# Output operands unsplit in DRAM, V's copies in the output phase, and an earlier set of early products in a hybrid attention and SSD layer

## The chip, the cores and the metric

The kernel runs on one core of a Trainium2 chip. A core has five engines with a queue of instructions each: PE (TensorE, matmuls; its weight loads are shown as PEld), DVE (VectorE), ACT (ScalarE), POOL (GpSimd) and SP (SyncE). SP, ACT and POOL also issue DMA transfers, and 16 DMA engines carry these out between DRAM, SBUF and DRAM again. The metric is the device time of one execution in microseconds, the lower the better. All data are float32.

## The reference

One decoder layer on x of 2048 tokens by 1024 features:

```python
proj = x @ w_in                            # 1024 -> 6672
q, k, v, z_att, z_ssm, xbc, dt_raw = split(proj)
# attention: 16 heads of 64, window of 128 steps, dilations 1, 4, 16, ALiBi bias
o_i, lse_i = dilated_window_attention(q, k, v, dilation_i)
y_att = sum_i softmax_i(lse)[i] * o_i
y_att = rms_norm(y_att * silu(z_att), g_att)
# SSM: causal convolution of width 4, Mamba-2 scan in chunks of 128
xs, B, C = split(silu(conv(xbc)));  dt = softplus(dt_raw + bias)
y_ssm = rms_norm((ssd(xs, dt, a, B, C) + d * xs) * silu(z_ssm), g_ssm)
out = concat(y_att, y_ssm) @ w_out         # 2048 -> 1024
return layer_norm(alpha * x + out)
```

## The kernel before

**Products in three parts.** A float32 product is made from three matmuls on a faster float32 type. Each operand a is split into a high part h (a cast, on ACT) and a low part l = a − h (a subtraction, on DVE or POOL), and h·h, h·l and l·h are added in PSUM. Who splits, when, and whether the split or the whole operand lies in DRAM is what much of this change is about.

**Stages.** First V is projected and stored (0 to 210 us of the profiled execution). Then 52 jobs follow, which make all other projections and the SSM half of the output projection. Then come the attention of eight head pairs (1481 to 2017 us) and the tail: the attention half of the output projection for 16 row blocks of 128 tokens, the norms and the result (to 2250 us).

**Jobs.** A job makes a 2 by 2 set of blocks by a scheme of seven products (a Strassen-like one, whose operands are sums and differences of blocks, named B11, B21, B22, T1 to T4). Each product is 12 matmuls of 128x512, so a job is 84. `products` (L391) issues them; `keep` (L402 to 405) copies a PSUM bank to an `ev` tile on ACT, one of six. The jobs go through the token halves: jobs 0 to 9 for half 0, jobs 10 to 31 for half 1, jobs 32 to 43 for half 0 again, and jobs 44 to 51 are the output jobs. A job's kind says which columns it makes: c (convolution channels), s (`z_ssm`), q, k, z (the attention gate) and o. In jobs 0 to 9 the order is c, s, c, s, c, s, c, s, c, c, and job 12 is an s job too. From about count 161 the SSM scan runs between the jobs.

**What sets the order.** PE, DVE, ACT and POOL run in the order in which the program is written; SP's order is found by the compiler's scheduler. Beside the seven products of a job the program puts small pieces of other work. `later[n]` (with its helpers `after` and `put`) is a list of functions for count n, and `flush()` (L386) runs those of the present count after each product. Job m covers counts 7m to 7m + 6. At 19 us a job, one count is 2.7 us.

**The pieces the change touches.** `token_sums` (L145) makes the sums for token half 1, and `output_side` (L270) those for the output jobs, from the weights `wout` and their gains. Both go through `in_steps` (L119): a difference, the high part on ACT (L127, L129), the low part on DVE (L134, L136) and a store of both (L139), each at a count of its own. The operands of the output jobs have four `wot` tiles, and POOL issues their stores. `output_load` (L307) loads the high and low parts of each of the seven operands, 1 MB each, on POOL (L320). `token_side` (L302) does the same for a new token half. `fin_zs` (L459) applies the gate function to a block of `z_ssm` and gathers it in a tile `ez`, of which there is one, and stores it (L468), twice in a job. `copy_v` (L580) copies V inside DRAM into the orders that dilations 4 and 16 read. `load_qk` (L783) loads queries and keys of a head pair. `fin_o` (L715) adds the rows of x (`row_load`, L707, on ACT's queue) to the SSM half.

**Attention and tail.** A pair has 24 half-steps, numbered (dilation, quarter, half). `scores` (matmul L953), `transposes` and `values` (L1002) run in a pipeline. While a pair runs, `combine` (L1064) adds the three dilations of the pair before with their weights: L1078 multiplies, L1087 adds, L1093 applies the gate, and L1098 and L1099 split the first three row blocks of the result (`uh`), which go to DRAM as `d_uh`. In the tail `product_early` (L1183) makes the part of row blocks 0 to 2 that needs no pair 7, from what `fetch_early` (L1131) brings back from `d_uh`; row block 3 is split in SBUF. `product_last` (L1199) adds pair 7. `gate` (L1260) multiplies pair 7's dilation 0 on POOL. `gather` and `weights` (L1047 to L1059) make the weights of the three dilations.

## Time and profile before

| | us |
|---|---|
| time, median of 3 runs | 2246.71 (2243.5 to 2250.11) |
| the profiled execution | 2251.73 |
| its span, first to last instruction | 2250.0 |
| PE busy | 2059.8 (92 % of the span) |
| DVE busy | 1487.2 (66 %) |
| ACT busy | 1216.9 (54 %) |
| POOL busy | 1184.1 (53 %) |

The mean granted clock of TensorE is 0.957 of full speed. The DMA engines moved 551.79 MB. Of the 16 engines' time, SP's queue took 35.7 %, POOL's 24.9 % and ACT's 14.1 %. A view by slices cuts the span into 40 equal parts and gives a busy share in tenths for each. A list of waits gives, for each engine, what ended its idle time: the engine, tile and line that waited, the releaser, then us in total, number and longest. A row of the timeline gives the start, the duration and, in brackets, the idle time ahead of the instruction and what released it.

### The profile page before, as it was taken

The page shows a single profiled execution, that of the slowest core. Times are in us where ns is not written, and L with a number is a line of the kernel's source. Part 1 is how long each engine was busy: PE and PEld are TensorE (multiplying, and loading weights), DVE is VectorE, ACT ScalarE, POOL GpSimd, SP SyncE. Part 2 cuts the span into 40 slices and gives each one's busy share as a digit, 9 for nine tenths or more (in the row PEclk, how much of TensorE's full clock was granted, in tenths as well). Part 3 has the DMA queues.
Part 4 walks back from the last instruction along what each step waited for, and adds up shares of the span by engine and source line. Part 5 has one row for each costly group of instructions (what it writes and reads, how often), then busy time and mean ns, then how long its engine had stood idle before and what let it go on. Part 6 is the DMA issues. An engine that isn't in the chain of part 4 may idle for free. (4 is left out here: it accounts for less than half of the span.)

```text
span 2250.0 us, 39433 instructions
## 1 busy us (share of the span) xinstructions
PE 2059.8 (92%) x13768; PEld 1707.0 (76%) x13768; DVE 1487.2 (66%) x3252; ACT 1216.9 (54%) x3131; POOL 1184.1 (53%) x980
## 2 busy tenths in 40 slices
PE   7999988879998999989999989979999999978798
PEld 7998766657887777767777868868887778866686
DVE  3432756837899678665656436548887888875666
ACT  3331443425555676666666534447887888862332
POOL 2113445745777667664555335532466677751544
PEclk9999999989999999999999999979999999998899
DMA  9999778886858868799788894453777778788342
GB/s 328 368 328 333 240 228 287 303 310 186 227 177 299 305 248 290 244 358 338 241 262 272 288 363 159 156 200 125 205 219 178 223 222 231 217 258 248 127 131 87
DMA packets 291799, 551.79 MB, mean 245 GB/s; under 512 B 77936, under 2 KB 145136, under 8 KB 274832
## 3 DMA queue, kind: packets, MB, share of 16 engines
q1 hardware_dynamic: 201536, 252.77, 35.7%
q0 software_dynamic: 36192, 194.46, 24.9%
q10 hardware_dynamic: 53872, 102.05, 14.1%
q8 instruction: 109, 1.79, 0.3%
q14 instruction: 90, 0.74, 0.1%
HBM read 359.39 MB, written 206.57 MB: 252 GB/s over the span
## 5 line engine op out<-in xcount | busy, mean ns | idle before, releaser
L351 POOL TENSOR_TENSOR w<-wr,w 128x512 fp32r<-128x512 f32 x287 | 432.2, 1520 | 291.5 <-ACT w L350 199.1
L969 ACT ACTIVATE P<-P,st 128x256 f32<-128x256 f32 (+1 forms) x768 | 345.1, 451 | 114.9 <-DVE st L961 114.4
L961 DVE CUSTOM_DVE_ANT_0 P<-S,tb 128x256 f32<-128x256 f32 (+1 forms) x768 | 235.3, 362 | 87.7 <-PE S L953 50.9
L404 ACT COPY ev<-pp 128x512 f32<-128x512 f32 x208 | 120.9, 581 | 254.8 <-PE pp L399 163.6
L350 ACT CAST w<-wr 128x512 fp32r<-128x512 f32 x287 | 171.1, 618 | 54.2 <-DVE wr L343 34.7
L343 DVE TENSOR_TENSOR wr<-wr 128x512 f32<-128x512 f32 x164 | 181.6, 1107 | 24.5 <-DMA wr<-w 12.6
L984 DVE COPY PT<-T 128x512 f32<-128x512 f32 (+1 forms) x304 | 196.6, 677 | 1.6 <-PE T L982 1.5
L982 PE MATMUL T<-ident,P 128*128 128x128 f32 x1200 | 179.6, 287 | 5.1 <-DVE PT L984 4.8
L1002 PE MATMUL N<-PT,v 128*64 128x128 f32 x2400 | 178.0, 286 | 3.4 <-DMA v<-d_v 3.1
L412 DVE TENSOR_TENSOR ev<-pp,ev 128x512 f32<-128x512 f32 x184 | 121.9, 682 | 74.2 <-PE pp L399 54.0
L1002 PEld LDWEIGHTS N<-PT,v 128*64 128x64 f32 x2400 | 130.7, 139 | 36.8 <-issue 25.7
L982 PEld LDWEIGHTS T<-ident,P 128*128 128x128 f32 x1200 | 130.6, 143 | 29.5 <-DVE PT L984 6.2
L1078 POOL TENSOR_TENSOR wb<-num,wb 128x2048 f32<-128x2048 f32 x21 | 96.4, 4591 | 102.7 <-DMA wb<-d_wd 73.0
L969 ACT ACTIVATION_READ_ACCUMULATOR P<-P,st 128x1 f32 x768 | 143.8, 187 | 0.0
L953 PE MATMUL S<-kh,qp 64*128 64x256 f32 (+1 forms) x1024 | 126.1, 306 | 0.0
L395 PE MATMUL pp<-TB22h,w 128*128 128x512 f32 x208 | 89.5, 430 | 36.5 <-ACT ev L404 34.4
L503 DVE SCALAR_TENSOR_TENSOR acc<-U,cw,acc 128x2048 f32<-128x2048 f32 x36 | 114.0, 3167 | 6.2 <-ACT acc L500 5.8
L452 DVE SCALAR_TENSOR_TENSOR ev<-ev 128x512 f32<-128x512 f32 x64 | 71.1, 1125 | 70.1 <-ACT ev L451 70.0
L953 PEld LDWEIGHTS S<-kh,qp 64*128 64x128 f32 x1024 | 88.8, 188 | 22.0 <-issue 20.5
L194 PE MATMUL pp<-vh,xh 128*128 128x256 f32 (+1 forms) x320 | 90.9, 290 | 15.8 <-ACT xh L217 15.8
L187 POOL TENSOR_TENSOR vl<-vraw,vh 128x256 fp32r<-128x256 f32 (+1 forms) x32 | 29.9, 938 | 130.9 <-ACT vh L186 107.7
L397 PE MATMUL pp<-TB22l,w 128*128 128x512 f32 x208 | 87.8, 422 | 5.2 <-DMA TB22l<-d_T0B 2.1
(487 smaller groups left out, 6106.6 us busy)
## 6 DMA issues: line engine op xcount, KB each, us to landing
wr<-w ACTq DMA_DIRECT2D x157, 256.0 KB
v<-d_v POOLq DMA_DIRECT2D x24, 1024.0 KB, 7.6
d_wc<-w SPq DMA_DIRECT2D x44, 512.0 KB
w<-d_wc POOLq DMA_DIRECT2D x44, 512.0 KB, 5.9
wb<-d_wd SPq DMA_DIRECT2D x42, 512.0 KB
csb<-d_cs ACTq DMA_DIRECT2D x32, 512.0 KB
st<-xT SPq DMA_DIRECT2D x23, 512.0 KB
d_v<-vt SPq DMA_DIRECT2D x16, 512.0 KB
```

Of the source, the lines that this page charges most:

```text
L343: tt = lambda o, a, b, op=OP.subtract: nc.vector.tensor_tensor(q[o], q[a], q[b], op=op)
L350: nc.scalar.copy(t[:, 0], q[nm])
L351: nc.gpsimd.tensor_tensor(t[:, 1], q[nm], t[:, 0].bitcast(F32), op=OP.subtract)
L404: nc.scalar.copy(e, ps)
L412: nc.vector.tensor_tensor(e, a, e, op=op)
L503: return lambda: nc.vector.scalar_tensor_tensor(acc[0], U[:, j:j + 16, :], cw[:, i, j:j + 1], acc[0], op0=OP.mult, op1=OP.add)
L953: nc.tensor.matmul(ov(sp[h][:, 256 * b:256 * b + w]), A["q"][d][x][hr, blk], kv(A["k"][y][hr]), start=(m == 0), stop=(m == 2))
L961: nc.vector.tensor_tensor_reduce(P[:, h, b, 256 - w:256], sp[h][:, c0:c0 + w], tab[:, h, tab.shape[2] - w:], 1.0, 3.0e38, OP.add, OP.min, ...
L969: nc.scalar.activation(p, p, AF.Exp, bias=stat(A, 0, d, h, blk), scale=-1.0, accum_out=stat(A, 1, d, h, blk))
L982: nc.tensor.transpose(tp[:, h, b], P[:, h, b, 128 * which:128 * which + 128], ident)
L984: nc.vector.tensor_copy(pt[:, :, bl[0]:2], tp[:, :, bl[0]:2])
L1002: nc.tensor.matmul(nm[64 * h:64 * h + 64, bq * 128:bq * 128 + 128], v[:, k, 64 * h:64 * h + 64], pts[which][:, h, b], start=(f or not whic ...
```

## The change

It has five parts. (1) The operands of the output jobs are stored whole (`d_U` has no high and low part any more). `output_side` makes each in one instruction into its own tile (13 tiles `wo`) and stores 256 KB on SP, at counts 45 to 67 instead of 38 to 66. `output_load` is now three functions: `load` brings an operand of 1 MB on SP into one of two staging tiles, `high` casts it on ACT (L316), `low` subtracts on DVE, or on POOL for operands 2 and 5 (L321). The token sums have two `to` tiles instead of three and two counts per sum. (2) `fin_zs` keeps both halves of a job in one `ez` tile and stores once, in runs of 512 bytes. (3) The 32 copies of V, 512 KB each, move from counts 3 to 149 to counts 318 to 356. (4) The queries of pair 0 are loaded at the first count of job 50 and the keys at the first count of job 51. Before, all four loads stood at the second count of job 51. (5) `d_uh` holds six pairs. The early products of row blocks 0 to 2 are of pairs 0 to 5; pair 6 stays in its tile `uh` and is multiplied with pair 7 in `product_last`. The steps of pair 6's `combine` move from half-steps (0,3,0), (1,0,0), (1,1,0), (1,2,0) of pair 7 to (1,0,1), (1,1,0), (1,2,0), (1,3,1).

POOL at the change of token half, ahead of job 10, before. L351 splits weights, L302 loads an operand of token half 1, L139 stores an operand of the output jobs:

```order
L139 DMA d_UB_143<-wot 128x2x512
L351 TENSOR_TENSOR w<-wr,w 128x512
L302 DMA TB11h<-d_T1B_116 128x2048
L302 DMA TB11l<-d_T1B_116 128x2048
L139 DMA d_UB_142<-wot 128x2x512
L351 TENSOR_TENSOR w<-wr,w 128x512 x2
L302 DMA TT1h<-d_T1T_119 128x2048
L302 DMA TT1l<-d_T1T_119 128x2048
L139 DMA d_UT_144<-wot 128x2x512
```

And now (L353 and L295 are the same two lines):

```order
L353 TENSOR_TENSOR w<-wr,w 128x512 x62
L295 DMA TB11h<-d_T1B_116 128x2048
L295 DMA TB11l<-d_T1B_116 128x2048
L353 TENSOR_TENSOR w<-wr,w 128x512 x2
L295 DMA TT1h<-d_T1T_119 128x2048
L295 DMA TT1l<-d_T1T_119 128x2048
```

The stores of the output operands and the copies of V have left POOL here.

POOL at the end of the output jobs, before. L790 loads queries and keys, L895 a table, L897 V:

```order
L351 TENSOR_TENSOR w<-wr,w 128x512 x53
L790 DMA qh<-d_qh_60 128x2048
L790 DMA kh<-d_kh_76 128x2048
L790 DMA ql<-d_ql_68 128x2048
L790 DMA kl<-d_kl_84 128x2048
L895 DMA tb_13252<-tabs 128x2x128
L897 DMA v<-d_v_100 128x16x128
```

And now (L584 copies V, L799 loads queries and keys, L902 and L904 are table and V):

```order
L799 DMA qh<-d_qh_60 128x2048
L799 DMA ql<-d_ql_68 128x2048
L584 DMA d_v_102<-d_v_100 16x8192
L353 TENSOR_TENSOR w<-wr,w 128x512 x3
L584 DMA d_v_102<-d_v_100 16x8192
L353 TENSOR_TENSOR w<-wr,w 128x512
L584 DMA d_v_102<-d_v_100 16x8192 x2
L353 TENSOR_TENSOR w<-wr,w 128x512
L584 DMA d_v_102<-d_v_100 16x8192
L353 TENSOR_TENSOR w<-wr,w 128x512
L799 DMA kh<-d_kh_76 128x2048
L799 DMA kl<-d_kl_84 128x2048
```

The queries stand ahead of the last copies and the keys right behind them, and the weight splits are cut into pieces by the copies.

POOL in the last pair, before. L1116 loads final weights, L1078 and L1087 are steps of pair 6's `combine`, L897 loads V for dilation 16:

```order
L1116 DMA kh<-d_wo 128x2048
L1116 DMA kl<-d_wo 128x2048
L1078 TENSOR_TENSOR wb<-num,wb 128x2048
L897 DMA v<-d_v_102 128x16x128
L1078 TENSOR_TENSOR wb<-num,wb 128x2048
L1087 TENSOR_TENSOR wb<-wb 128x2048
L1116 DMA qh<-d_wo 128x2048
```

And now (seven lines further down in the file):

```order
L1123 DMA kh<-d_wo 128x2048
L1123 DMA kl<-d_wo 128x2048
L904 DMA v<-d_v_102 128x16x128
L1123 DMA qh<-d_wo 128x2048
L1123 DMA ql<-d_wo 128x2048
L1123 DMA v<-d_wo 128x2048
L1321 DMA num<-d_za_99 128x2048
L1085 TENSOR_TENSOR wb<-num,wb 128x2048 x2
L1094 TENSOR_TENSOR wb<-wb 128x2048
```

V's load and the loads of the final weights stand ahead of the first step of `combine`.

The diff, without the parts that the text above tells in full:

```diff
-    d_U = {n: dtile(f"d_U{n}", [2, 128, 4, 512]) for n in ("B11", "B21", "B22", "T1", "T2", "T3", "T4")}
+    d_U = {n: dtile(f"d_U{n}", [128, 4, 512]) for n in ("B11", "B21", "B22", "T1", "T2", "T3", "T4")}
-    d_uh = dtile("d_uh", [3, 128, 2, 7, 128])
+    d_uh = dtile("d_uh", [3, 128, 2, 6, 128])
...
+            def item(nm, make):
+                def f():
+                    make(tile_(nm))
+                    nc.sync.dma_start(d_U[nm][:, k], R[nm])
+                return f
...
+                (0, "B11", lambda o: act(o, R["11"], AF.Copy, scale=col(gc, 0))),
+                (0, "B22", lambda o: act(o, R["22"], AF.Copy, scale=col(gc, 1))),
+                (1, "B21", lambda o: act(o, R["21"], AF.Copy, scale=col(gc, 1))),
+                (2, "T1", lambda o: stt(o, R["12"], col(gc, 0), R["B11"], op0=OP.mult, op1=OP.subtract)),
+                (3, "T3", lambda o: stt(o, R["12"], col(gn, 0), R["B22"], op0=OP.mult, op1=OP.add)),
+                (3, "T2", lambda o: tt(o, R["B22"], R["T1"], op=OP.subtract)),
+                (4, "T4", lambda o: tt(o, R["T2"], R["B21"], op=OP.subtract))):
+                put(b + n, item(nm, make))
...
+            def load(i):
+                stage[i] = qq.tile([128, NR, NJ], F32, name="q" + "hl"[i % 2], bufs=1).rearrange(
+                    "p (k r) j -> p k (r j)", k=4)
+                nc.sync.dma_start(stage[i].rearrange("p k t -> p (k t)"), d_U[LEFT[i]].rearrange("p k t -> p (k t)"))
+            def high(i):
...
+                for h in range(2):
+                    nc.scalar.copy(T[i][0][:, 2 * h:2 * h + 2], stage[i][:, 2 * h:2 * h + 2])
+            def low(i):
+                for h in range(2):
+                    s = slice(2 * h, 2 * h + 2)
+                    (nc.gpsimd if i in (2, 5) else nc.vector).tensor_tensor(
+                        T[i][1][:, s], stage[i][:, s], T[i][0][:, s].bitcast(F32), op=OP.subtract)
...
+            n0 = 7 * 43
+            for i in range(7):
+                c = n0 + 3 * i // 2 if i else n0 - 4
+                put(c, lambda i=i: o_high(i))
+                put(c + 1, lambda i=i: o_low(i))
+                if i < 5:
+                    put(c + 1, lambda i=i: o_load(i + 2))
+            o_load(0)
+            o_load(1)
...
-            for j in range(32):
-                later.setdefault(4 * j + (3 if j < 13 else 25), []).append(lambda j=j: copy_v(1 + j // 16, j % 16))
+                put(7 * 45 + 3 + 5 * j // 4, lambda j=j: copy_v(1 + j // 16, j % 16))
...
-                    after(1, lambda: load_qk(pairs[0]))
+                    later[count[0]].insert(0, lambda: load_qk(pairs[0], 1))
+                if m + 2 == len(jobs):
+                    after(0, lambda: load_qk(pairs[0], 0))
...
-            nc.gpsimd.dma_start(SP[n].rearrange("p (a c t) -> p a c t", a=2, t=128)[:, :, 0:7], d_uh[n])
+            nc.gpsimd.dma_start(SP[n].rearrange("p (a c t) -> p a c t", a=2, t=128)[:, :, 0:6], d_uh[n])
...
-                mm(pss[hf], hf, lhs, range(6), True, False)
-            for hf in range(2):
-                mm(pss[hf], hf, lhs, [6], False, True)
+                mm(pss[hf], hf, lambda e: (part(t, 0)[:, e, :], part(t, 1)[:, e, :]), range(7 if n == 3 else 6),
+                   True, True)
...
-                mm(pss[hf], hf, lambda e: (e7[:, 0, n], e7[:, 1, n]), [7], True, True)
+                mm(pss[hf], hf, lambda e: (two[e - 6][:, 0, n], two[e - 6][:, 1, n]), [7] if n == 3 else [6, 7],
+                   True, True)
...
-                        step = ((0, 3, 0), (1, 0, 0), (1, 1, 0), (1, 2, 0))
+                        step = ((1, 0, 1), (1, 1, 0), (1, 2, 0), (1, 3, 1))
```

121 lines of the change are left out of this document (45 added, 76 removed).

## The prediction

> **What bounds the kernel now.** I read first the page's slices, then the waits, and then cut the span into the jobs that the change touches.
>
> ```profile
> PE   7999988879998999989999989979999999978798
> ...
> PEclk9999999989999999999999999979999999998899
> ```
>
> Each digit is 1/40 of the span (56.25 us). PE is busy nearly everywhere, so time is lost only in the few slices below 9. They are the early jobs (slices 6 to 9), the start of the attention (slice 27) and the tail (from slice 37). The list of all waits names what stands there:
>
> ```profile
> ACT ez L465 <- DMA d_zs<-ez: 45.3, 7, 12.4
> ...
> PE pp L395 <- ACT ev L404: 42.6, 12, 9.1
> ...
> ACT wot L127 <- DMA d_UB<-wot: 22.2, 6, 8.7
> ```
>
> The columns are us in total, times, longest. ACT waits for a *store*: its result tile (`ez`, `wot`) is still being written to DRAM. PE in turn waits for ACT, because the PSUM bank of the next product is emptied by ACT's copy L404, which is queued behind the waiting instruction. The stretches that hold these jobs, with one quiet job ahead as a measure, are:
>
> ```profile
> 232.00:251.00 19.00, 19.00 (x85) 15.72 (x85) 12.97 (x16) 10.41 (x18) 10.21 (x10) 1.00 0.70 242
> 251.00:279.00 28.00, 22.84 (x89) 18.28 (x88) 24.70 (x41) 12.77 (x22) 11.58 (x9) 0.88 0.70 214
> 299.00:330.00 31.00, 22.11 (x85) 17.68 (x85) 17.47 (x20) 10.42 (x19) 11.99 (x9) 0.83 0.71 214
> 349.00:379.00 30.00, 20.88 (x86) 16.82 (x85) 19.79 (x20) 12.39 (x24) 18.06 (x18) 0.83 0.83 277
> 400.00:427.00 27.00, 21.60 (x87) 17.12 (x86) 23.09 (x22) 14.35 (x26) 16.94 (x16) 0.94 0.82 262
> 446.00:493.00 47.00, 29.88 (x85) 20.54 (x85) 9.97 (x13) 10.28 (x17) 21.36 (x27) 0.78 1.02 389
> 512.00:538.00 26.00, 21.58 (x84) 17.29 (x83) 15.34 (x13) 11.91 (x21) 14.30 (x14) 0.87 0.75 213
> 1276.00:1302.00 26.00, 21.71 (x90) 17.52 (x89) 5.49 (x10) 6.30 (x11) 8.78 (x12) 0.93 1.08 390
> 1321.00:1347.00 26.00, 21.68 (x86) 16.85 (x85) 7.81 (x11) 8.47 (x15) 8.88 (x8) 0.93 0.98 375
> 1349.00:1481.00 132.00, 131.89 (x579) 108.24 (x577) 72.50 (x79) 57.99 (x100) 64.50 (x49) 1.00 0.50 166
> ```
>
> Columns: stretch, us, busy time of PE, PEld, DVE, ACT, POOL, granted clock, DMA share, GB/s. A job is 84 matmuls of 128x512; the first row does it in 19.0 us with no gap at full clock. Everything above 19.0 is loss, and it includes the lower clock that follows a gap. The losses in row order are 9, 12, 11, 8 (jobs 2, 4, 6, 8), 28 (job 10, the change of token half), 7 (job 12), 7 and 7 (jobs 42 and 44, into the output jobs). The seven output jobs behind (last row) lose nothing, with the DMA half idle.
>
> **Part by part, 1: output operands unsplit, one `ez` tile.** Before, each operand of the output product is split on ACT and DVE at counts 38 to 66 of the schedule, and POOL stores 512 KB per piece. Now 256 KB per piece go out on SP at counts 45 to 67, from 13 tiles instead of 4; an `ez` store happens once per job, in 512-byte runs instead of 256-byte ones.
>
> ```profile
> ACT wot L129 <- DMA d_UT<-wot: 10.9, 7, 4.0
> ...
> 317.11 1.15 ACT L465 ACTIVATE ez<-ev 128x512 f32<-128x512 f32 x2 [12.38 <-DMA d_zs<-ez]
> ...
> 525.70 0.63 ACT L465 ACTIVATE ez<-ev 128x512 f32<-128x512 f32 x1 [9.77 <-DMA d_zs<-ez]
> ```
>
> The waits of ACT named so far (`ez` up to 45.3, `wot` 22.2 + 10.9) cover the 40 us lost in jobs 2, 4, 6 and 8. The second `ez` tile of a job waited for the first one's store, 12.38 us; now the next user of the tile is the next z job, over 19 us later, so that wait is gone. With 13 tiles no `wot` piece waits for its own store. I take −35 of the 40. The bounds are −42 (also small losses of the jobs between) and −22 (about half, if other ACT work such as the token sums, now with two tiles and not three, takes over the place). Job 12 has one `ez` wait, 9.77 us: −7 (−7 to 0).
>
> **2: change of token half (job 10).** POOL loads 14 pieces of 1 MB for job 10, and before, the last 512 KB operand stores stood between them on POOL.
>
> ```profile
> 435.58 0.57 POOL L302 DMA_DIRECT2D TB11h<-d_T1B  x1
> ...
> 488.80 0.79 PE L397 MATMUL pp<-TT3l,w 128*128 128x512 f32 x1 [1.99 <-DMA TT3l<-d_T1T]
> ```
>
> First issue to last piece used: 53 us for 14.7 MB, with the engines at share 1.02. So it is bound by bytes: what goes away is the four last stores, 2.1 MB, at 389 GB/s 5.4 us, and POOL's wait ahead of the first issue, some 5 us (the splits in front follow ACT, which no longer stalls). −10, from −6 to −13; the rest of the 28 stays, since the loads still begin when the old half's tiles come free.
>
> **3: V copies moved.** 32 copies of 512 KB, DRAM to DRAM, are 16.8 MB.
>
> ```profile
> d_v<-d_v POOLq DMA_DIRECT2D x16, 512.0 KB, 5.5
> ```
>
> Their removal from counts 3 to 149 frees DMA time up to job 21: −3 (0 to −8) for store waits there. They now run at counts 318 to 356, in the output jobs 45 to 51. In the last window row those jobs move 166 GB/s at share 0.50, so full share is about 332 GB/s; the copies are 51 us of it, put into some 109 us that had half free, 54 us. It fits, but barely: share about 0.97. What hides it is the idle half; where the x rows or split weights of a job come late behind copies, the price shows. The two rows at share 1.08 and 0.98 lost 7 us per job, most of it for reasons of part 4. I take +6, from 0 to +25 (half of seven times 7).
>
> **4: output operands split at use.** Seven 1 MB loads on SP into two staging tiles, then two ACT casts and two subtractions each (DVE; POOL for i = 2 and 5) of 128x1024. Half the bytes of before, but new work:
>
> ```profile
> L218 DVE TENSOR_TENSOR xl<-st,xh 128x1024 fp32r<-128x1024 f32 x15 | 18.5, 1231 | 38.8 <-ACT xh L217 38.8
> ...
> L1255 POOL TENSOR_TENSOR kh<-kh,wb 128x1024 f32<-128x1024 f32 x8 | 23.5, 2938 | 0.6
> ...
> 1289.92 0.59 ACT L404 COPY ev<-pp 128x512 f32<-128x512 f32 x1 [6.73 <-DMA d_qh<-ev]
> ```
>
> DVE: 10 × 1.23 = 12.3 us; POOL: 4 × 2.94 = 11.8 us; ACT about as DVE. In the two windows these engines are busy 5 to 9 of 26 us, so the work itself is hidden. Not hidden is a late load: if a staging tile is not full, ACT waits in `high`, and behind it L404 and so PE; on SP a load that waits for its staging tile holds the q and k stores behind it, which free `ev` (the 6.73 us wait above is of that kind). Against it stands that half of the operand bytes leave this stretch, at 390 GB/s 19 us of DMA (7 of 14 MB). Bounds −6 (one of the two losses goes) to +14 (both double); I take +4, since two staging tiles are few.
>
> **5: start of the attention.** Queries are now loaded in job 50, keys at the first count of job 51.
>
> ```profile
> 1483.52 1.20 POOL L897 DMA_DIRECT2D v<-d_v  x1 [8.29 <-ACT ev L718]
> ...
> 1489.32 0.48 PE L953 MATMUL S<-kl,qh 64*128 64x128 f32 x2 [7.59 <-DMA kl<-d_kl]
> 1489.95 6.87 DVE L719 SCALAR_TENSOR_TENSOR ev<-x,ev 128x512 f32<-128x512 f32 x1 [5.81 <-DMA x<-xc]
> 1497.00:1518.00 21.00, 20.70 (x136) 16.32 (x136) 11.26 (x70) 13.94 (x65) 0.85 (x2) 0.50 0.21 62
> 1518.00:1526.00 8.00, 8.00 (x56) 6.35 (x56) 3.25 (x18) 4.08 (x19) 0.00 (x0) 0.50 0.06 17
> ```
>
> The wait for `kl` (7.59) goes: keys land before job 51 ends. The last x row also comes sooner (5.81), since no q and k traffic stands beside it, and L719 no longer runs beside POOL's casts of `qp`. Late next is V of pair 0, issued at 1483.52 behind the last output row, and 7 us under way. The first scores start about 1485 instead of 1497, the first values product a little after: −11. Bounds −8 (V decides alone) and −22 (also 10 us of the half clock, below). The Trainium skill ("GPSIMD Engine Reference", 1. Specifications) says that POOL shares its SBUF interfaces with VectorE, in contention with DVE instructions that have two SBUF inputs. This trace agrees, 6.87 us for L719; it speaks against `low` of i = 2 and 5 on POOL, and by it part 4 would be an estimated 2 to 6 us dearer, inside its bounds.
>
> **6: last pair and tail.** Pair 6's weighting moves two to three half-steps later, so the load of V for dilation 16 no longer stands behind it on POOL:
>
> ```profile
> 1984.39 4.57 POOL L1078 TENSOR_TENSOR wb<-num,wb 128x2048 f32<-128x2048 f32 x1 [17.31 <-DMA wb<-d_wd]
> ...
> PE N L1002 <- DMA v<-d_v: 3.1, 1, 3.1
> ```
>
> −3. The tail's early products now need only pairs 0 to 5, long stored:
>
> ```profile
> 2030.85 4.52 POOL L1260 TENSOR_TENSOR num<-num 128x2048 f32<-128x2048 f32 x1
> 2031.67 3.76 DVE L1047 TENSOR_TENSOR mm<-cm 128x32 f32<-128x32 f32 x1 [15.56 <-DMA cm<-d_st]
> 2034.06 0.76 PE L1172 MATMUL S<-kh,num 128*128 128x512 f32 x1 [16.72 <-DMA num<-d_uh]
> ...
> 2056.65 1.07 ACT L1197 COPY qp<-S 128x512 f32<-128x512 f32 x2 [20.39 <-DMA wb<-d_wd]
> ...
> 2121.73 0.79 PE L1172 MATMUL S<-kh,num 128*128 128x512 f32 x1 [11.27 <-ACT num L1142]
> 2034.00:2076.00 42.00, 41.39 (x171) 33.19 (x171) 23.85 (x22) 9.57 (x16) 2.64 (x3) 0.95 0.80 237
> 2124.00:2250.00 126.00, 116.80 (x498) 93.98 (x498) 83.26 (x120) 36.33 (x51) 60.46 (x22) 0.96 0.36 119
> ```
>
> PE's 16.72 us wait goes, yet I count it at almost nothing. What ends the tail's first part is pair 7's own chain: statistics (2031.67, 15.56 us behind their store), weights, ACT held till 2056.65 by its 20.39 us wait, then the product and the row blocks, where PE waits 11.27 us again. Work begun sooner on PE only makes PE wait longer there. From that chain only the 3.76 us go, which a 128x32 instruction costs beside L1260 on POOL: −3. Pair 6 adds 18 matmuls to the late part, 18 × 0.23 = 4.1 us, which those waits mostly hide: +1.5. Behind 2124 PE is busy 116.80 of 126 and nothing changes. Tail and pair 7: −4.5, from −16 (the early begin pays after all) to +4 (the 18 matmuls are not hidden).
>
> **Sum.** −35 − 7 − 10 − 3 + 6 + 4 − 11 − 4.5 = −60.5 us on the span of 2250.0, so 2189.5. The profiled execution took 2251.73, 5 us above the median of 2246.71, and I take the difference from the median: 2246.7 − 60.5 = **2186 us**.
>
> **Rivals.** (a) *The stalls are partly replaced.* For it speaks that ACT has several kinds of store waits behind one another in the early jobs, so that the next one takes over; part 1 then brings −22, part 4 costs +14, part 3 +10: 2186 + 13 + 10 + 4 = 2213. Against it: the stores become half as large and the tiles three times as many. (b) *The clock returns at once at the start of the attention.* In the two rows of 1497 to 1526 the granted clock is 0.50 while PE is busy 28.70 of 29 us. With the full clock ACT would bound that work, 13.94 + 4.08 = 18 us, so 11 us go: 2175. Against it: this trace shows 29 us of half clock under unbroken work. The Trainium skill ("TensorE: Matmul & The Clock Gate", What's actually happening) says that about 3.4 us of sustained activity give the full clock back. By that rule the result would be this rival's; the trace does not agree, as the rows above show, so it has a small chance. (c) *The early begin pays in full:* the tail is PE-bound from 2017 on, 16.7 − 4.1 = 12.6 us instead of 1.5: 2175. Against it: PE's 11.27 us wait at 2121.73. (d) *The copies starve the output jobs; slower.* Its place is jobs 45 to 51, its mechanism that x rows and weights queue behind the V copies at a share near 1. The three rows at share 0.98 to 1.08 lost 7, 7 and 28 us, on average 14; seven such jobs cost 98 instead of 6: 2278. It decides from about 9 us per job on, where 66 us eat the gain. Against it: on average 3 % of the DMA stays free, and the copies are spaced one per 3.4 us.
>
> **Chances.** Forecast 0.58, (a) 0.19, (b) 0.14, (c) 0.05, (d) 0.04. A measurement of this kernel tells about 0.3 %, 6.7 us, from no change. Faster by more: 0.93 (all but (d) and a far tail of (a)); within: 0.03; slower: 0.04. Range 2158 to 2222: down to the bounds −42 and −22 of parts 1 and 5 with the rest as taken, less 10; up over (a) with another 9 us of copies.
>
> **What would show it.** Part 1: no `ez` or operand wait on ACT of over 2 us, windows of jobs 2 to 8 at 19 to 21 us. Part 2: job 10 near 37 us. Part 3: share 0.9 to 1.0 in the output jobs and PE still without gaps; gaps before L395 that name x rows or weights show (d). Part 4: ACT waits in the casts of the staged loads. Part 5: first score product right behind job 51, V of pair 0 the last to come. Part 6: no wait for `d_uh`, a longer one at the later row blocks, and the same distance from the end of the attention to the end. It is wrong if early jobs keep more than 20 of their 40 us, or if the output jobs lose over 4 us each.

## The result and the profile after

The changed kernel takes 2225.44 us (median of 4 runs, 2220.32 to 2228.08) against 2247.08 us. The ratio is 0.990, with an interval of 0.988 to 0.993. It is faster, by 21.6 us, but the forecast was 60.5 us, and the time lies above the top of the range (2222). The profiled execution has a span of 2226.3 us against 2250.0.

The stretches of the changed kernel that answer to those shown of before, with the same columns (stretch, us, busy PE, PEld, DVE, ACT, POOL, granted clock, DMA share, GB/s), are job 2, job 4, job 10, job 12, job 42, job 44, and jobs 45 to 51 together:

```profile
252.00:280.00 28.00, 22.94 (x92) 18.50 (x91) 24.52 (x41) 12.08 (x22) 10.01 (x8) 0.88 0.57 177
299.00:318.00 19.00, 19.00 (x86) 15.78 (x85) 12.83 (x17) 9.10 (x18) 9.83 (x8) 1.00 0.84 280
413.50:455.00 41.50, 27.40 (x85) 19.97 (x84) 5.53 (x10) 8.39 (x13) 16.36 (x20) 0.81 1.01 383
475.00:494.00 19.00, 19.00 (x85) 15.77 (x84) 14.74 (x13) 10.57 (x17) 14.08 (x13) 1.00 0.66 205
1230.00:1249.00 19.00, 19.00 (x86) 15.76 (x85) 3.64 (x7) 6.73 (x11) 5.22 (x7) 1.00 0.95 345
1272.00:1304.00 32.00, 22.06 (x85) 17.57 (x84) 20.35 (x14) 15.28 (x23) 21.16 (x10) 0.79 0.47 164
1304.00:1456.00 152.00, 137.02 (x589) 110.70 (x587) 82.28 (x85) 60.49 (x104) 84.13 (x85) 0.98 0.80 279
```

Jobs 4, 12 and 42 run without a gap now. Job 2 still loses 8 us, and job 44 more than before. The last row is the surprise: seven output jobs that lost nothing before lose 18 us, and the DMA engines are busy only 0.80 of that time. The whole account, from the first matmul of each job and the first values product of each pair, in both traces:

| stretch | before, us | after, us | difference | forecast |
|---|---|---|---|---|
| V stage and jobs 0 to 9 | 445.6 | 413.5 | −32 | −35 |
| jobs 10 and 11 | 66.2 | 61.3 | −5 | −10 |
| job 12 | 26.3 | 19.0 | −7 | −7 |
| jobs 13 to 41 | 738.1 | 736.3 | −2 | −3 |
| jobs 42 to 44 | 70.3 | 73.8 | +3.5 | +4 |
| jobs 45 to 51 | 134.3 | 152.3 | +18 | +6 |
| end of job 51 to the first values product | 21.9 | 11.9 | −10 | −11 |
| pairs 0 to 6 | 453.8 | 460.2 | +6.4 | none |
| pair 7 | 60.7 | 68.2 | +7.5 | −3 |
| tail | 232.8 | 229.7 | −3 | −1.5 |

Three rows carry 29 of the 37 us that are missing on the span: the output jobs (12), pairs 0 to 6 (6.4) and pair 7 (10.5). Job 10 (5) and the early jobs (3) stand behind them. The waits that stand in those places in the changed kernel are, of DVE over the whole span, and of ACT in job 2 (timeline):

```profile
DVE ev L719 <- DMA x<-xc: 29.8, 9, 6.3
```

```profile
272.19 0.62 ACT L137 CAST to<-st 128x512 fp32r<-128x512 f32 x1 [8.87 <-DVE st L143]
```

In the output jobs it is the x rows that come late, on DVE; ACT's next use of the `ev` tiles and PE's bank stand behind that. In job 2 ACT waits for DVE in a token sum, not for a store. Pair 7 has a wait that was not there before (timeline rows of POOL, ACT and PE):

```profile
1966.64 4.58 POOL L1085 TENSOR_TENSOR wb<-num,wb 128x2048 f32<-128x2048 f32 x1 [22.17 <-ACT num L1016]
...
1980.53 4.50 POOL L1085 TENSOR_TENSOR wb<-num,wb 128x2048 f32<-128x2048 f32 x1
```

```profile
1985.06 0.59 ACT L1019 COPY num<-N 128x512 f32<-128x512 f32 x1 [13.19 <-POOL wb L1085]
```

```profile
1986.20 0.47 PE L989 MATMUL T<-ident,P 128*128 128x128 f32 x1 [8.10 <-ACT P L976]
```

ACT may not write pair 7's result for dilation 16 into the `num` tile until POOL has read pair 6's from it. POOL's first multiplication begins 38 us into pair 7 (1928.4); before it began 28 us into it (1984.39 against 1956.4). Why it is later stands on SP's queue, where the weights go to DRAM (L1065, L1058 before) and are loaded back once they have landed (L1071, L1064), first of the changed kernel, then of before:

```profile
1940.93 0.36 SPq L1065 DMA_DIRECT2D d_wd<-cm  x1
1955.84 1.32 SPq L1071 DMA_DIRECT2D wb<-d_wd  x2
```

```profile
1969.34 0.36 SPq L1058 DMA_DIRECT2D d_wd<-cm  x1
1977.03 1.12 SPq L1064 DMA_DIRECT2D wb<-d_wd  x2
```

The small store took 14.9 us to land instead of 7.7. In the changed kernel POOL does not wait for it ahead of its loads, and has issued 7 MB of them from 1935 to 1945: five final weights, V and the gate. Before, two weights were on the way at that time.

The row of POOL names an ACT copy as its releaser, where other traces name the loaded weights, so the link to the store rests on a comparison of traces and on the run below that moves the loads. In nine traces with the late steps and the loads ahead of them, the store was 11.0 to 16.5 us under way and the first multiplication began 38 to 44 us into pair 7. In three of the kernel before it was 5.5 to 8.0 us, and 26 to 29 us.

### The profile page after: what moved, and what is told of

The parts are those of the page before. It is cut to its first block, busy times and chain, and to the rows that moved or that the text cites. A ratio compares the mean times of both kernels' runs of the same rounds, so it can differ in the third digit from the quotient of the medians.

```text
span 2226.3 us, 39336 instructions
## 1 busy us (share of the span) xinstructions
PE 2056.8 (92%) x13768; PEld 1708.8 (77%) x13768; DVE 1460.6 (66%) x3234; ACT 1219.3 (55%) x3125; POOL 1173.1 (53%) x942
## 5 line engine op out<-in xcount | busy, mean ns | idle before, releaser
L353 POOL TENSOR_TENSOR w<-wr,w 128x512 fp32r<-128x512 f32 x287 | 436.6, 1538 | 284.4 <-ACT w L352 201.2
L991 DVE COPY PT<-T 128x512 f32<-128x512 f32 (+1 forms) x304 | 197.0, 678 | 12.5 <-PE T L989 12.5
L345 DVE TENSOR_TENSOR wr<-wr 128x512 f32<-128x512 f32 x164 | 169.0, 1031 | 22.6 <-DMA wr<-d_us 9.6
L1085 POOL TENSOR_TENSOR wb<-num,wb 128x2048 f32<-128x2048 f32 x21 | 96.1, 4577 | 110.2 <-DMA wb<-d_wd 72.7
L454 DVE SCALAR_TENSOR_TENSOR ev<-ev 128x512 f32<-128x512 f32 x64 | 73.5, 1161 | 68.8 <-ACT ev L453 68.7
L397 PE MATMUL pp<-TT2h,w 128*128 128x512 f32 x208 | 84.0, 404 | 15.0 <-ACT ev L406 15.0
L397 PE MATMUL pp<-TB21h,w 128*128 128x512 f32 x208 | 84.1, 404 | 9.9 <-ACT ev L406 9.9
```

Source lines behind the costliest of these rows:

```text
L345: tt = lambda o, a, b, op=OP.subtract: nc.vector.tensor_tensor(q[o], q[a], q[b], op=op)
L353: nc.gpsimd.tensor_tensor(t[:, 1], q[nm], t[:, 0].bitcast(F32), op=OP.subtract)
L397: nc.tensor.matmul(ps, w[:, 0, k], th[:, k], start=start and k == 0, stop=False, skip_group_check=not start)
L991: nc.vector.tensor_copy(pt[:, :, bl[0]:2], tp[:, :, bl[0]:2])
```

## The experiments

Each starts from the changed kernel. The stretches below were read from one trace each, in us; a time in the text is the median of its runs.

| kernel | jobs 0 to 2 | 3 to 9 | 12 to 21 | 45 to 51 | pairs 1 to 6 | pair 7 | tail |
|---|---|---|---|---|---|---|---|
| before, three traces | 69.0, 69.1, 72.7 | 166.5, 164.5, 159.1 | 205.0, 202.9, 199.7 | 134.3 in each | 382.0, 382.6, 381.6 | 60.7, 62.7, 57.7 | 232.8, 231.8, 235.4 |
| changed, two traces | 69.0, 68.8 | 133.8 | 197.9, 197.6 | 152.3, 153.6 | 387.3, 389.4 | 68.2, 69.2 | 229.7, 232.0 |
| V copies early | 69.8 | 140.4 | 196.9 | 135.9 | 383.9 | 73.6 | 230.2 |
| old steps in pair 7 | 68.4 | 133.8 | 200.2 | 154.6 | 393.7 | 57.6 | 236.2 |
| token sums moved | 60.9 | 133.8 | 196.9 | 156.6 | 385.9 | 69.5 | 229.7 |
| two `ez` stores | 68.3 | 133.8 | 196.0 | 148.7 | 382.8 | 71.7 | 229.4 |
| V copies in short runs | 66.8 | 133.8 | 198.6 | 141.2 | 390.8 | 69.1 | 229.5 |
| final weights later | 66.6 | 133.8 | 196.8 | 155.8 | 390.6 | 58.5 | 230.0 |
| queries and keys late | 68.0 | 133.8 | 199.5 | 145.6 | 395.8 | 68.8 | 230.3 |
| two `ez` stores, copies early | 67.0 | 149.8 | 197.1 | 134.9 | 386.6 | 68.9 | 229.8 |
| the same, short runs | 68.9 | 136.9 | 202.6 | 135.9 | 380.5 | 74.0 | 230.6 |
| combination, copies half and half | 61.7 | 133.8 | 217.6 | 135.4 | 384.9 | 64.3 | 229.5 |
| the same, dilation 4 in short runs | 61.2 | 133.8 | 209.8 | 135.9 | 383.8 | 61.5 | 230.4 |
| the same, keys ahead of combine | 61.2 | 133.8 | 206.5 | 136.2 | 394.2 | 67.0 | 231.1 |
| combination, all copies short, output jobs | 60.7 | 133.8 | 194.9 | 139.7 | 383.9 | 65.1 | 230.4 |

**The copies of V back in the early jobs.**

```diff
-put(7 * 45 + 3 + 5 * j // 4, lambda j=j: copy_v(1 + j // 16, j % 16))
+put(4 * j + (3 if j < 13 else 25), lambda j=j: copy_v(1 + j // 16, j % 16))
```

> The changed kernel with the 32 copies of V put back to counts 3 to 149; everything else as changed. Theory (the copies are what costs jobs 45 to 51, +17.6 us against the kernel before, by making x rows late: DVE waits 29.3 us in 8 waits for them): jobs 45 to 51 go back to 19.2 us each, no wait of L719 for x of over 1 us, and the early jobs stay as they are since the 512 KB operand stores no longer stand there: 2225 - 17 = 2208 us. Rival 1 (the split of the output operands at use, or the weights' loads, make these jobs long): jobs 45 to 51 stay at 20 to 27 us, 2225. Rival 2 (the copies crowd the early jobs wherever they stand): jobs 45 to 51 are mended but jobs 4 to 9 and 20 to 22 lose 5 to 10 us: 2214 to 2219.

It took 2220.45 us (2214.49 to 2222.36). Jobs 46 to 50 are back at 19.1 us each, so the copies are what cost in the output jobs, and rival 1 falls. Jobs 5 to 8 lose 6.6 us, so rival 2 has its share: the theory and rival 2 hold together.

**The old steps of pair 6's combine.**

```diff
-step = ((1, 0, 1), (1, 1, 0), (1, 2, 0), (1, 3, 1))
+step = ((0, 3, 0), (1, 0, 0), (1, 1, 0), (1, 2, 0))
```

> The changed kernel with pair 6's steps back at half-steps (0,3,0), (1,0,0), (1,1,0), (1,2,0) of pair 7; the early products stay with six pairs. Theory (with the later steps POOL issues five 1 MB loads ahead of its wait; they stand in the way of the store of the weights d_wd, 14.9 us instead of 7.7 under way, so the steps end 10 us later in pair 7 and ACT waits 13.2 us for a num tile that POOL still reads, PE 8.1 us, and the clock halves): the 8.1 us wait and the half clock go, a wait for V of about 3 us comes back, pair 7 is 7 us shorter: 2218. Rival 1 (the wait is there anyway, since the num tile is shared): pair 7 keeps it, 2225. Rival 2 (what is won there is lost in the tail, whose chain sets the end): pair 7 shorter, tail longer by the same, 2224.

Pair 7 took 57.6 us instead of 68.2, and the tail 236.2 instead of 229.7. Together that is 293.8, as in the three traces of before (293.5, 294.5, 293.1), against 297.9 and 301.2 with the change. Both the theory and rival 2 are met in part: of the 10.6 us won in pair 7 the tail takes back 6.5. What the tail loses is PE's wait for `d_uh`, which is 13.2 us here, against 3.1 in the changed kernel. Counted from the start of pair 7, the fetch lands at the same time in both (70.9 and 71.3 us), so a shorter pair 7 only waits longer behind it. The time was 2219.44 us (2211.37 to 2232.27), a spread too wide to tell the runs apart by their times.

**Token sums outside job 2.**

```diff
-token_sums(k, 7 + 8 * k)
+token_sums(k, (4, 20, 27, 33)[k])
```

> The changed kernel with the four token sums begun at counts 4, 20, 27, 33 instead of 7, 15, 23, 31, so that none of their steps falls into job 2. Theory (job 2 keeps 8.4 us of loss because ACT's casts of the token sums wait for DVE, which works off 16 us of the step-size chain there, and L406 is queued behind them): job 2 takes 19 to 21 us, 2217 to 2219. Rival (DVE's chain itself holds the result of a product in L414, and so PE): job 2 stays above 25 us, 2224 or 2225.

Job 2 took 19.7 us instead of 27.4. The window over it in this trace:

```profile
252.00:272.00 20.00, 20.00 (x90) 16.57 (x89) 17.03 (x32) 9.47 (x16) 6.92 (x6) 1.00 0.33 99
```

PE has no gap. The time, 2221.78 us (2215.87 to 2227.2), shows little of it, because jobs 22 to 41 and 45 to 51 of this trace lost some us more; the cause of the loss in job 2 itself is shown.

**Two `ez` stores per job as before.** The tile of one half, written again by the second half, and runs of 256 bytes:

```diff
-            t = cp.tile([128, 16, 2, 8, 8], F32, name="ez", bufs=1)
+            t = {}
...
+                if ci not in t:
+                    t[ci] = cp.tile([128, 16, 8, 8], F32, name="ez", bufs=1)
...
-                if (ci, q) == (1, 0):
+                if q != ci:
```

> The changed kernel with the z_ssm part as before: two stores per job in runs of 256 bytes, the second half of a job using the tile of the first. Theory (the wait for that store was the main cause in jobs 4, 6, 8 and 12): these four lose again 6 to 11 us each, about 33 us: 2255 to 2260. Rival (the operand stores on POOL and the splits on ACT were the main cause, and made the ez store slow as well): job 12 and the early jobs lose 2 to 4 us each, 10 to 15 in all: 2235 to 2240.

It took 2223.83 us (2215.78 to 2230.75), and jobs 3 to 9 exactly what they take in the changed kernel. Theory and rival both fall: with the splitting and large stores of the operands and the copies out of the way, the `ez` tile needs no change at all. The next runs ask which of them had made the `ez` store slow.

**Two `ez` stores and the copies early, then the same with the copies in short runs.** The second differs from the first in

```diff
-nc.gpsimd.dma_start(d_v[d][b], dap(d_v[0], o * D, [[128 * D, (4, 16)[d - 1]], [D, (32, 8)[d - 1]], [1, D]]))
+G, N = (4, 16)[d - 1], (32, 8)[d - 1]
+for h in (0, 512):
+    nc.gpsimd.dma_start(dap(d_v[d], b * 128 * D + h, [[N * D, G], [D, N], [1, 512]]),
+                        dap(d_v[0], o * D + h, [[128 * D, G], [D, N], [1, 512]]))
```

The bytes are the same, but a run is 2 KB long. In the traces' record of DMA packets the copies were packets of 64 KB for dilation 4 (128 of them, 3.0 us each in the changed kernel) and of 32 KB for dilation 16 (256, 1.5 us each). With the short runs they are packets of 4 KB (4096, 0.19 us each). The text calls the two forms long and short runs.

> The changed kernel with the z_ssm part as before (two stores of 256-byte runs, second half waiting for the first) and the copies of V at counts 3 to 149 as before. With either alone jobs 3 to 9 took 133.4 us (two stores) and 140.2 us (copies early), the kernel before 166.4, the changed one 133.4. Theory (the 12 us under way of an ez store in the kernel before came from the 512 KB operand stores of POOL and ACT's splits, which are gone in both): 140 to 145 us, no ez wait over 4 us, within 5 us of the time with the copies early alone, 2220. Rival (the copies, with 64 KB runs, held the 256-byte runs of the ez stores): ez waits of 8 us and more come back, jobs 3 to 9 take 155 to 165 us, about 2240.

> The changed kernel with two ez stores per job and the copies of V at counts 3 to 149, as in an earlier run (jobs 3 to 9 149.8 us, waits for ez stores 33.6 us in 7), but with the copies in 2 KB runs. Theory (what made the ez store late in the kernel before were the long runs of the copies, behind which its 256-byte runs stand): ez waits fall to 12 to 18 us as without the copies (12.5), jobs 3 to 9 take 134 to 139 us. Rival (the bytes of the copies): ez waits stay above 28 us, jobs 3 to 9 above 145.

ACT's waits for `ez`, from the list of waits of the run with two stores alone, with the early copies, and with these in short runs (before: 45.3, 7, 12.4):

```profile
ACT ez L467 <- DMA d_zs<-ez: 12.5, 5, 3.1
```

```profile
ACT ez L467 <- DMA d_zs<-ez: 33.6, 7, 7.9
```

```profile
ACT ez L467 <- DMA d_zs<-ez: 17.9, 4, 7.7
```

Jobs 3 to 9 took 133.8, 149.8 and 136.9 us; the times were 2231.01 (2228.59 to 2240.51) and 2224.11 us (2223.68 to 2224.53). The first run lies between its two cases. The second meets its theory: the same bytes at the same counts cost jobs 3 to 9 3 us instead of 16 when the runs are short. Jobs 12 to 21, which hold most of the other copies, took 202.6 us with short runs and 197.1 with long ones, so the short form was not better everywhere. What remains up to the 159 to 167 us of before belongs to what else the change does in these jobs, the splitting and 512 KB stores of the output operands and the new counts of the token sums. No run put these back alone.

**The copies in the output jobs, in short runs.** The edit to `copy_v` is the one above.

> The changed kernel with the copies of V in the same place and of the same bytes, but each as two transfers of half the columns, so that a run is 2 KB and not 32 or 64 KB. In the changed kernel jobs 45 to 48, whose copies have runs of 64 KB, lose 1.6, 3.2, 8.1 and 0.9 us, jobs 49 to 51, with runs of 32 KB, 1.4, -0.1 and 2.5. Theory (an x row of 2 KB runs queues on each DMA engine behind the long runs of a copy, so it is late although the engines are only 0.59 to 0.84 busy): the waits of L719 for x (29.3 us in 8) fall below 8 us, jobs 45 to 51 lose 0 to 5 us in all instead of 17.6, 2211 to 2215. Rival (the bytes as such: x rows share the bandwidth with 16.8 MB of copies): waits for x stay at 20 us or more, 2225, or more since short runs are less efficient.

It took 2214.63 us (2213.57 to 2225.57). Jobs 45 to 51 took 141.2 us, against 148.7 to 156.6 in six traces with long runs at these counts (145.6 in a seventh, which loads pair 0's queries and keys later). DVE's waits for x rows, in this trace over the output jobs:

```profile
DVE ev L722 <- DMA x<-xc: 19.6, 9, 5.9
```

They fell less than the theory says (29.3 to 19.6, not below 8), and 7 us of loss stay. By the times of the jobs the long runs are the larger part, about 11 of 18 us, and the bytes the rest. How long an x row is under way can be worked out from its issue and the last of the 16 updates of its semaphore. The median in jobs 45 to 51 is 3.0 to 3.3 us in the kernel before, 6.5 in the changed kernel and 6.7 here, so the usual delay comes from the bytes and not from the long runs. What the short runs change is the late rows: 9 of 30 took over 8 us in the changed kernel, the longest 12.9; here it is 3 of 28, the longest 10.0, and before 2 of 28.

**The final weights later.** Three final weights and the gate, 4 MB on POOL, one half-step later:

```diff
-                    elif at == (1, 0, 0):
+                    elif at == (1, 0, 1):
                         for e, name in enumerate(("qh", "ql", "v"), 2):
```

> The changed kernel with the loads of three final weights and the gate (4 MB, on POOL) one half-step later, (1,0,1) instead of (1,0,0), so that they stand behind the first multiplication of pair 6's combine and not ahead of it. With the late steps pair 7 took 68.2, 73.7, 69.5 and 71.7 us in four traces, with the old steps 57.7, but there the tail behind it took 236.2 instead of 229.4 to 230.1. Theory (what delays the steps is the 4 MB in the way of the store of d_wd, 14.9 us under way): that store lands within 9 us, ACT's 13.2 us wait for num falls below 4 us, pair 7 takes 58 to 61 us, and the tail stays below 233: 2214 to 2218. Rival 1 (the steps themselves, placed later in POOL's order, are the delay): pair 7 stays at 66 us or more. Rival 2 (the weights are then late for the early products): pair 7 shorter, tail 236 or more, 2222 or more.

Pair 7 took 58.5 us and the tail 230.0, so neither rival holds in this trace. SP's queue and ACT's longest wait in pair 7 show the mechanism:

```profile
1948.06 0.36 SPq L1065 DMA_DIRECT2D d_wd<-cm  x1
1956.22 3.69 SPq L1071 DMA_DIRECT2D wb<-d_wd  x6
```

```profile
ACT num L1019 <- POOL wb L1085: 5.3, 1, 5.3
```

The store of the weights lands in 8.2 us again, and ACT waits 5.3 us where it waited 13.2. The size is less sure than the direction: in three later runs that contain the same edit (leaving out the one that also moves the keys) the store took 10.1 to 12.1 us and pair 7 took 61.5 to 65.1. The time was 2221.17 us (2215.65 to 2226.05), above the 2214 to 2218 of the theory; other stretches of this trace are longer (jobs 22 to 41 by 6 us), as they were in others.

**A combination, with the copies half and half.** Token sums and final weights as above, and

```diff
-put(7 * 45 + 3 + 5 * j // 4, lambda j=j:
+put(84 + 4 * j if j < 16 else 318 + 5 * (j - 16) // 2, lambda j=j:
```

> A combination: the copies for dilation 4 (64 KB runs) in counts 84 to 144, those for dilation 16 in the output jobs, spread over counts 318 to 355; token sums outside job 2; the final weights one half-step later. Theory (each of the three losses stands by itself): job 2 19.7 us, jobs 45 to 51 within 5 us of 134, jobs 12 to 21 lose 3 to 4 us, pair 7 58 to 61 us: 2225 - 8 - 13 + 3 - 7 = 2200 us. Rival (what is won is lost at the next wait or by the half clock): 2210 to 2220.

> The changed kernel with four edits: the copies of V for dilation 4 in 2 KB runs (two transfers each) at counts 84 to 144, those for dilation 16 (32 KB runs) at counts 318 to 355; token sums outside job 2; the final weights one half-step later in pair 7. Theory (the 64 KB runs are what cost, 17.6 us in jobs 45 to 51 of the changed kernel and 20 us in jobs 12 to 21 of the combination before): jobs 12 to 21 take 196 to 202 us instead of 217.6, jobs 45 to 51 135 to 136, job 2 19.7, pair 7 58 to 65: 2196 to 2204 us. Rival (the bytes in jobs 12 to 21 cost in any form): jobs 12 to 21 stay at 212 or more, 2216 to 2220.

The first took 2218.95 us (2215.53 to 2221.86), the time of its rival. Jobs 45 to 51 hold only the copies for dilation 16, at half the rate, and take 135.4 us, no more than with no copies there (135.9). Long runs of 32 KB thus cost nothing at that rate; run length and rate were not separated. Jobs 12 to 21, which now hold those for dilation 4 with 64 KB runs, lose 20, where I expected 3 or 4. PE's waits there:

```profile
PE pp L401 <- POOL w L353: 9.0, 3, 6.3
PE pp L397 <- ACT ev L406: 8.1, 3, 3.6
```

The weights of the next job come late here, through POOL's split. In the second run the same copies have 2 KB runs: 209.8 us for jobs 12 to 21 (206.5 in the next run, which has the same copies), 2210.47 us in all (2209.91 to 2215.0). That lies between theory and rival: short runs give back 8 to 11 of 20 us, and the rest stays with the bytes in this place.

**Keys ahead of combine.** In the last combination the loads of the next pair's queries and keys stand ahead of combine's first multiplication:

```diff
+if pr < 7 and at == (1, 0, 0):
+    load_qk(pairs[pr + 1])
 if pr and at in step:
     combine(pairs[pr - 1], step.index(at))
```

> The same combination, and in each pair the loads of the next pair's queries and keys ahead of combine's first multiplication on POOL, and not behind it. Between 1 and 3 of the pairs 1 to 6 took 65 to 71 us in every trace so far, the others 62.5, and each long one holds 3.4 to 10 us of half clock. Theory (PE's wait of 0.5 to 3.4 us for the last key load at the start of a pair sets off the half clock): no wait for keys of over 0.3 us from pair 1 on, pairs 1 to 6 take 375 to 377 us in all instead of 382 to 394, 5 to 15 us less than the combination without it. Rival 1 (the loads now stand in the way of the combine's weights, as in pair 7): pairs get longer, 2205 or more. Rival 2 (the half clock comes from other gaps): no wait for keys, but still one to three long pairs.

2223.41 us (2221.3 to 2224.72), 13 us worse. PE's waits in the attention:

```profile
PE N L1015 <- DMA v<-d_v: 7.3, 2, 5.0
PE T L995 <- DVE PT L997: 6.8, 6, 1.7
PE N L1015 <- DVE PT L997: 5.4, 3, 4.3
PE S L966 <- DMA kl<-d_kl: 4.0, 1, 4.0
```

The waits for keys are gone from pair 1 on (the 4.0 us is pair 0's), but V and DVE are late instead, and pairs 3 and 5 took 72.5 and 70.5 us. The theory falls. The time is that of rival 1, though the waits name V and DVE, and not the combine's weights that it names. Two long pairs without a wait for keys are also what rival 2 expects. So the run shows that the earlier loads cost more than they save, and does not tell the two rivals apart.

**The combination with all copies short, in the output jobs.**

> The combination with all copies of V in the output jobs in 2 KB runs, instead of half of them in counts 84 to 144. From the runs so far: jobs 45 to 51 141 us (135 there), jobs 12 to 21 197 to 198 (196 to 202 there): 2197 to 2205 us, within 5 us of the combination with split places. If jobs 45 to 51 take 150 us or more, short runs do not help by themselves and the first result with them (141.2) was chance.

This is the fastest, and as expected: 2200.35 us (2195.4 to 2204.16), ratio 0.978 (0.975 to 0.981) to the kernel before. Jobs 45 to 51 took 139.7 us; in a window over them the DMA engines are busier than in the changed kernel, and PE loses less:

```profile
1293.00:1436.00 143.00, 138.63 (x603) 112.63 (x602) 91.47 (x86) 60.22 (x104) 103.18 (x115) 0.99 0.88 297
```

**Both kernels profiled again, and the loads of queries and keys put back.** The last run has the four loads at the second count of job 51, in the old order.

> The kernel before, profiled again, to see which of its times are the same in every execution. In its first trace pairs 1 to 6 took 382.0 us with one pair of 67.4 and the others near 62.8, pair 7 60.7, the tail 232.8, the 22 us ahead of the first values product 21.9. Theory (the half clock in pairs 1 to 6 is chance in both kernels): pairs 1 to 6 take 382 to 394 us here too, as in the traces of the changed kernel and its variants. Rival (the change makes it more frequent): 378 to 383. Pair 7 60 to 62 and the tail 232 to 234 in either case.

> As the run before it: a third profile of the kernel before. Theory (chance): pairs 1 to 6 together between 380 and 394, not the same as in the other two. Rival: 378 to 383 in all three.

> The changed kernel profiled again. Expected the same within 0.3 us where no wait is near (jobs 3 to 9, 12, 13), jobs 45 to 51 148 to 157 us, pair 7 68 to 72, tail 229 to 231; pairs 1 to 6 anything from 382 to 394 if the half clock there is chance, the same pairs long as before (4 and 6) if it has a place.

> The changed kernel with the four loads of pair 0's queries and keys back at the second count of job 51, in the old order. Theory (these loads set the start of the attention): from the end of job 51 to the first values product 20 us or more, as in the kernel before (21.9), instead of 10.8 to 12.4. Rival (V of pair 0 and the half clock set it, and the loads only need to land before V does): 11 to 16 us.

Single times: 2248.87 and 2242.26 us for the kernel before, 2233.52 for the changed one, 2236.35 with the loads put back. The kernel before has 381.6 to 382.6 us in pairs 1 to 6 in all three traces, which is the rival's case. The changed kernel has 387.3 and 389.4, and its variants (without the one that moves the keys) 380.5 to 395.8. The long pairs of the changed kernel are 4 and 6 in both traces (67.5 and 67.4 us, then 69.9 and 67.0), and again in six of its variants, so their place is not mere chance. In the last run the first values product comes 17.7 us behind job 51, between the theory (20 or more) and the rival (11 to 16), and PE waits for the keys there:

```profile
PE S L958 <- DMA kl<-d_kl: 8.0, 1, 8.0
```

So 6 of the 10 us at the start of the attention come from these loads. The other 4 were not separated. But jobs 45 to 51 took 145.6 us in this run, 7 to 8 less than in the two traces of the changed kernel. From the start of job 45 to the first values product it is 163.3 us against 164.2 and 165.4: beside the copies, the earlier loads win almost nothing in all, as far as one trace tells. Without copies in these jobs the same stretch took 147.9 us, against 156.2 before.

## Why the prediction was wrong, step by step

**Part 3 failed, by 12 us.** The step "It fits, but barely: share about 0.97" priced the copies by their bytes, +6. They cost 18 at a share of only 0.80. The price was not the room for the bytes but the delay of the small transfers beside them: an x row was under way 6.5 us instead of 3, and 9 of 30 took over 8. At the same place and with the same bytes, 2 KB runs cost 7, and there 3 of 28 rows took over 8 us. Some of the 18 may belong to the loads of part 5, which the forecast let run beside the copies for nothing: in the one trace with these later, jobs 45 to 51 lost 11, in the six with long runs and early loads 14 to 22. Rival (d) named the place and the late x rows, and its price by job (7 to 28 us) was far too high; 2.6 us per job was real.

**Part 6 failed, by 10 us, in pair 7.** The step "so the load of V for dilation 16 no longer stands behind it on POOL" was right (that wait is gone) and stopped one question short: what POOL now issues early, and what that meets. Its loads held up the small store on which the combine waits, and the combine held a tile that ACT needs. Moving 4 MB behind the first multiplication took 9.7 us from pair 7 in one trace and 3 to 7 in three others.

The tail's number was right, partly by luck. PE's wait for `d_uh` fell from 16.7 to 3.1 us, and the tail by 3, since later waits grew (list of waits from the end of the attention on; before 11.3 and 2.7 us):

```profile
PE S L1179 <- ACT num L1149: 15.4, 2, 11.4
PE N L1185 <- DVE tb L1156: 5.4, 2, 4.8
PE S L1179 <- DMA num<-d_uh: 3.1, 1, 3.1
```

The step, that the early products no longer wait for pair 6's store, came about: POOL waited 10.4 us for that store ahead of the fetch and now does not. But counted from the start of pair 7 the fetch lands only 6 us sooner (71.3 against 77.5 us). The other 7.5 us by which PE's wait shrank are those by which pair 7 grew; with the old steps and a short pair 7 the wait was 13.2 us.

**Part 1 was right in size, partly by luck, and partly wrong in cause.** −32 of −35. But "The waits of ACT named so far ... cover the 40 us lost in jobs 2, 4, 6 and 8" is not so for job 2, whose 8 us are token sums behind DVE's step-size chain. And the `ez` waits, the largest of ACT's waits for a store, needed no repair of their own: in the changed kernel the old tile brings 12.5 of the 45.3 us back, at no cost to PE. The gain there belongs about as much to part 3's move of the copies, which I had given 3 us: with the old `ez` stores and the copies back, jobs 3 to 9 lost 16 of their 33 us again.

**Part 2 was too high.** The T loads began at 401.04, 12.5 us ahead of job 10, where they had begun 10.1 us ahead of it (435.58 against 445.7). Job 10 took 39.3 to 41.7 us in the traces of the changed kernel and its variants, not 37: −5 to −8 of the forecast −10, at the same share near 1.

**Part 4 was right** (+3.5 for +4), with both effects: job 42 lost its wait, 43 and 44 gained new ones. **Part 5 was right at the start** (−10 for −11), though in the one trace that tells, the output jobs paid about as much for it.

**What no step foresaw is that pairs 1 to 6 take some 5 us longer.** More of them runs at half clock: 13.7 us in each trace of the changed kernel, 3.4 to 6.8 in those of before. Work at half clock takes twice the time, so this is an estimated 3 to 5 us. It follows short gaps, one at the start of pair 4 in the changed kernel:

```profile
1784.10:1787.60 3.50, 1.98 (x22) 1.74 (x24) 1.43 (x10) 0.98 (x6) 3.50 (x1) 0.99 0.49 150
1787.60:1794.40 6.80, 6.80 (x54) 5.69 (x50) 3.38 (x12) 3.14 (x15) 6.71 (x4) 0.50 0.01 2
```

In the first row PE is busy 1.98 of 3.5 us, with a wait of 1.67 us for the last key load in it; in the second it works without a pause at half clock. Why this happens more often in the changed kernel, whose pairs 1 to 5 are issued in the same order, stays open: the three traces of before agree within 1 us, those of the changed kernel and its variants spread over 15. Rival (b) did not come about: the half clock at the start lasts 34.1 us.

**The kernel's own spread.** Four runs of one kernel differ by 3 to 21 us among themselves, so that single losses of 5 to 10 us were settled here by stretches of the traces and not by medians.

## What to carry to other kernels

An idle half of the DMA engines is not free room: price a background copy by what its long runs do to the small transfers that share the engines, and try it in short runs and at a lower rate. Short runs did not make it free: they took away the latest of the small transfers, not their usual delay. When a wait is taken from a queue that issues DMAs, list what the queue now issues early and which small transfer, and which tile behind that, will meet it. A list of waits names who is held, not the cause; the largest wait for a store here shrank to a harmless one without its own repair. When a wait shrinks, ask from which end: here half of it went because the work ahead of it had grown.

## What the runs showed of the hardware

Runs of 64 and 32 KB in a DRAM to DRAM copy delayed transfers with short runs in other queues, at a mean share of 0.6 to 0.8: jobs 3 to 9 took 149.8 us with long runs and 136.9 with 2 KB runs, jobs 45 to 51 about 153 and 141, jobs 12 to 21 217.6 and 209.8. The x rows of the output jobs, 256 KB in packets of 2 KB, were under way 3.0 to 3.3 us (median) with no copies beside them, 6.5 to 7.5 in seven traces with long runs and 6.7 in two with short ones; over 8 us took 9 to 11 of some 30 rows with long runs, and 3 with short ones. The Trainium skill ("DMA: Bandwidth & Descriptors", Queues, rings and completion order) says that an engine goes round its queues and drains a whole packet from one before it switches. The late rows beside packets of 3.0 us agree with that, and the equal medians do not tell for or against it. The traces show the packets' sizes and times, but not which of the 16 engines ran a packet, so the turns themselves are not shown. The same page's rules for kernel authors favour large transfers; here the halves of 256 KB cost POOL more issues (39.0 us for 64 against 18.4 for 32) and the kernel was still faster with them in the output jobs (2214.63 against 2225.44 us).

The granted clock changes in steps of 3.4 us: the record of the clock has spells at half clock of 3.4, 6.8, 10.2, 13.7, 17.1, 20.5, 30.7, 34.1, 37.5 and 41.0 us, and one other in each trace, which runs past the end of the kernel. In the rows of pair 4 above, a stretch of 3.5 us with PE busy 57 % of it stands ahead of a spell of 6.8 us. At the start of the attention PE was at half clock for 34.1 us, and busy 31.43 of them:

```profile
1459.90:1494.00 34.10, 31.43 (x208) 24.68 (x208) 16.02 (x95) 19.14 (x88) 12.86 (x21) 0.50 0.42 121
```

The Trainium skill ("TensorE: Matmul & The Clock Gate", What's actually happening) has the same window, 3413 ns, and says that one busy window brings the full clock back; on that the two rows of half clock here disagree.
